# Two matmul stages of a convolution layer: groups of outputs in another turn, operands prepared tile by tile, block sums on VectorE

## The chip, the cores and the metric

One core of a Trainium2 chip. The metric is the device time of one launch in microseconds (us). TensorE is PE, VectorE DVE, ScalarE ACT, GpSimd POOL; SyncE (SP) only issues DMAs, and so does ACT's queue for some stores.

## What is computed

One layer over 2048 tokens of width 1024, float32, DEPTH = 1, so the mixer is the short convolution:

```python
h = modulate(rms_norm(x, norm_gains[i, 0]), sh_m, sc_m)   # shift, scale, gate from c @ ada_w
bcv = h @ w_in; gate_b, gate_c, v = jnp.split(bcv, 3, axis=-1)
h = (gate_b * conv3(gate_c * v)) @ w_out                  # three taps, causal, per channel
x = x + g_m * rms_norm(h, norm_gains[i, 1])
h = swiglu(modulate(rms_norm(x, norm_gains[i, 2]), sh_f, sc_f))   # w_gate_up, silu(g)*u, w_down
x = x + g_f * rms_norm(h, norm_gains[i, 3])
```

## The kernel before

**Stages.** The tokens are two halves u = 0, 1 of 1024. Each half goes through four matmul stages: `in` (w_in), `out` (w_out), `gu` (w_gate_up), `down` (w_down). The order in the program is in0, out0, in1, out1, gu0, down0, gu1, down1. `in1` does not read what `out0` makes: it is the other half of the tokens.

**Seven products.** A stage works in groups of outputs. A group is a 2 by 2 block product (two quarters of 512 tokens by two blocks of output columns, each over two halves of the inner dimension) done with seven products P1 to P7 in place of eight. The left operands are sums of quarters: A11, A12, A22, S1, S2, S3, S4 (`FEATURES`, line 40). The right ones are sums of weight blocks 11, 12, 21, 22. Each operand is split in two parts: a rounded one ("high", on ACT, type fp32r) and the rest ("low", on VectorE), and a product of 128 inner rows is three matmuls of 128x512. A group's product is a slot: 12 matmuls, in `out` 9 + 3 for P1 and P2. `slots` is the order of all of them, and everything else is hung on slot numbers: a list of events (`schedule`), chores that come back (`later`, `run`), and the supply of weights (`supply`, lines 830 to 844), which runs ahead of the products by so many places: 9 for the loads of blocks, 7 for their sums, 5 for the high part, 4 for the low part, 5 for weights kept whole (line 31). All engines run in the order in which the program was written.

**Weights.** In `in0`, the groups of feature blocks j = 1 and 2 also store their seven split operands in DRAM; `in1` reads them back whole ("kept") for these j and makes those of j = 0 and 3 again from blocks ("unkept"). In `gu0` and `gu1` the first three of 22 groups are kept, the other 19 unkept. `Blocks.sum` (lines 319 to 328) makes the four block sums of an unkept group; they run on POOL (`G`), those of the first three groups of `in0` on VectorE (`V`). While `in` runs, the weights of three groups of `gu` are prepared too (`Between`).

**Order of groups.** A group of `in` is one of c, C, b (the two input halves of the gated product, and the output gate) for a j. `in1` takes j in the order 1, 2, 0, 3, three groups each; the first three groups go in lockstep, the rest one after another. When group b of a j is done, `sums` (lines 650 to 667) forms S1 to S4 of the convolution's result on VectorE and POOL and stores all seven operands of that j in DRAM (`y_d`), tile k = j of four.

**Operands.** `loaded` (lines 747 to 778) brings the operands of `out` and `down` back: a DMA 6 slots before the first use, the high part 4, the low part 3 before. `normalized` (lines 730 to 745) makes those of `in1`, `gu0` and `gu1` from x: load, scale by the norm's factor (VectorE), shift (ACT), sums and splits, each as one instruction over four tiles (128x2048) where it can.

**Chores near the change.** `norm_of_rows` loads x again by rows (tiles `xr`, 16 loads of 256 KB for `in1`), squares on ACT; it starts 66 and 40 slots before `in1`. `mods_later((2, 3), ...)` loads `ada` tiles (32 of 256 KB) and reduces each against silu(c) on VectorE; it starts 8 slots into `out0`, one step every 1.25 slots. `after_out` computes x + gate * norm during the next stage (tiles `zz`, `xx`, and `nq` on POOL). SBUF is held in pools by tile size: 16 tiles of 8 KB per partition, 13 of 2 KB for raw blocks, 9 temporaries (line 32); a DMA or an instruction that fills a tile waits for the last user of that buffer.

Of the kernel before, what the change touches and what calls it, by code (L numbers as in the profile page):

```python
# [13 lines left out]
ALU = mybir.AluOpType  # L14
# [17 lines left out]
NBIG, NWP, NRAW, NTMP, NRB = 16, 7, 13, 9, 2  # L32
# [14 lines left out]
def hybrid_conv_layer(  # L47
# [255 lines left out]
    class Blocks:  # L303
# [193 lines left out]
    class Group:  # L497
# [85 lines left out]
        def ready_b(self, c):  # L583
# [12 lines left out]
            if {"12", "21"} <= self.done:  # L596
                run(sums(t, y_d[ph.u], self.i, f"{self.name}s"))
# [52 lines left out]
    def sums(t, d, k, name):  # L650
# [12 lines left out]
        store(("S2", s2))  # L663
# [23 lines left out]
    class Features:  # L687
# [59 lines left out]
    def loaded(ph, slots, first):  # L747
# [61 lines left out]
    for s in slots:  # L809
# [5 lines left out]
        else:  # L815
            b = of.setdefault((ph.name, s.n), Blocks(ph.kind, s.grp, ph.name == "in0" and s.n < LEAD))
# [404 lines left out]
    for ph in phases[1:]:  # L1221
# [28 lines left out]
    schedule(first["out0"] + 8, lambda: run(mods_later((2, 3), 1.25)))  # L1250
# [88 lines left out]
```

## Time and profile before

| | |
|---|---|
| Three runs | 2028.06, 2029.80, 2031.02 us, median 2029.8 us |
| The profiled execution | 2027.7 us, of which the span from the first to the last instruction is 2025.9 us |
| PE busy | 1949.8 us (96%), 8460 matmuls |
| VectorE, ScalarE, POOL busy | 71%, 43%, 33% |
| Granted TensorE clock, mean | 0.988 of full |
| DMA | 463.19 MB, mean 229 GB/s |

PE counts as busy also while its clock is low, so what a stretch loses is seen from its number of matmuls rather than from its busy time. In names, `in0P` is a PSUM bank of stage in0, `in7P` a pair of split weights of group 7's weights, `in7b` raw blocks of it, `out0S` an operand S of out0; numbers at the end of names are left out, and so S1 to S4 read alike. Almost every instruction goes through one helper, so its line is L75.

### The profile page before, as it was taken

How to read it: one execution, taken by the hardware profiler on the slowest of the kernel's cores; microseconds unless marked ns; L12 is line 12 of the kernel's file. 1: busy time of each engine (PE TensorE's matmuls, PEld its weight loads, DVE VectorE, ACT ScalarE, POOL GpSimd, SP SyncE). 2: the span in 40 equal slices, each digit the busy share in tenths (PEclk: the TensorE clock that was granted, in tenths of full speed). 3: DMA queues.
4: the chain of work that ended last, by engine and by line, in shares of the span. 5: the costliest groups of instructions: out<-in, count | busy, mean ns of one | idle time of the engine just before them, and what ended most of it. 6: DMA issues, size and time to landing. Idle time of an engine off the chain costs nothing.

```text
span 2025.9 us, 25058 instructions
## 1 busy us (share of the span) xinstructions
PE 1949.8 (96%) x8460; PEld 1583.4 (78%) x8460; DVE 1436.3 (71%) x1894; ACT 862.8 (43%) x1394; POOL 668.6 (33%) x436
## 2 busy tenths in 40 slices
PE   5899998999889999999999999999999999999998
PEld 2578786778777778887888888887888888888886
DVE  5887887887989685698757656667767555565456
ACT  5533446633333653343333435544333333344452
POOL 0134531302542233357856421111444343311010
PEclk9999998999999999999999999999999999999999
DMA  9269959879766775477656788567746234185644
GB/s 392 73 262 343 353 189 352 318 258 344 240 221 213 277 270 187 140 232 252 227 184 219 258 278 308 197 247 258 224 158 222 94 122 138 68 310 214 208 148 148
DMA packets 206193, 463.19 MB, mean 229 GB/s; under 512 B 23024, under 2 KB 38512, under 8 KB 199152
## 3 DMA queue, kind: packets, MB, share of 16 engines
q1 hardware_dynamic: 178416, 396.18, 56.5%
q10 hardware_dynamic: 27648, 65.41, 8.5%
q8 instruction: 66, 1.08, 0.2%
q14 instruction: 63, 0.52, 0.1%
HBM read 328.33 MB, written 133.17 MB: 228 GB/s over the span
## 4 chain that ended last, share of the span: by engine, by line
PE 72%; DVE 13%; DMA 7%; issue 4%; ACT 3%; SPq 0%; POOL 0%; ACTq 0%; POOLq 0%; DVEq 0%
PE gu1P L75 20%; PE gu0P L75 16%; PE down0P L75 10%; PE down1P L75 9%; PE in0P L75 7%; PE in1P L75 6%; PE out0P L75 2%; PE out1P L75 2%; DVE zz L75 1%; DMA xr<-x_d 1%; DMA xx<-xt_d 1%; DVE xx L75 1%; DVE ada L75 1%; DVE gu0a L75 1%; DVE in1y L75 0%
## 5 line engine op out<-in xcount | busy, mean ns | idle before, releaser
L75 DVE TENSOR_TENSOR gu1a<-gu1P,gu1a 128x512 f32<-128x512 f32 x63 | 43.4, 690 | 93.6 <-PE gu1P L75 86.8
L75 DVE TENSOR_TENSOR gu0a<-gu0P,gu0a 128x512 f32<-128x512 f32 x63 | 43.2, 688 | 60.4 <-PE gu0P L75 55.4
L75 POOL TENSOR_TENSOR down0q<-down0q,down0q 128x512 f32<-128x512 f32 x14 | 26.0, 1855 | 154.4 <-ACT down0q L75 154.3
L75 POOL TENSOR_TENSOR down1q<-down1q,down1q 128x512 f32<-128x512 f32 x10 | 16.1, 1613 | 148.6 <-ACT down1q L75 148.5
L75 ACT COPY gu1a<-gu1P 128x512 f32<-128x512 f32 x42 | 24.5, 586 | 89.8 <-PE gu1P L75 78.3
L75 DVE CUSTOM_DVE_ANT_0 ada<-ada,c 128x512 f32<-128x512 f32 x80 | 62.5, 791 | 0.2 <-ACT c L75 0.2
L75 ACT COPY gu0a<-gu0P 128x512 f32<-128x512 f32 x42 | 24.5, 584 | 72.4 <-PE gu0P L75 64.6
L75 ACT COPY gu1g<-gu1P 128x512 f32<-128x512 f32 x24 | 14.1, 587 | 90.9 <-PE gu1P L75 90.9
L75 POOL TENSOR_TENSOR gu1a<-gu1a 128x512 f32<-128x512 f32 x11 | 19.5, 1774 | 89.6 <-DVE gu1g21s L75 24.7
L75 DVE TENSOR_TENSOR gu1g<-gu1P,gu1g 128x512 f32<-128x512 f32 x24 | 16.6, 690 | 45.1 <-ACT gu1g L75 43.8
L75 POOL TENSOR_TENSOR nq<-nq,nq 128x512 f32<-128x512 f32 x28 | 46.5, 1660 | 2.6 <-ACT nq L75 2.4
L75 ACT COPY gu0g<-gu0P 128x512 f32<-128x512 f32 x24 | 14.1, 586 | 73.3 <-PE gu0P L75 73.3
L75 POOL TENSOR_TENSOR out1q<-out1q,out1q 128x512 f32<-128x512 f32 x14 | 24.1, 1724 | 59.1 <-ACT out1q L75 59.0
L75 DVE TENSOR_TENSOR gu0g<-gu0P,gu0g 128x512 f32<-128x512 f32 x24 | 16.6, 690 | 32.2 <-ACT gu0g L75 31.6
L75 POOL TENSOR_TENSOR out0q<-out0q,out0q 128x512 f32<-128x512 f32 x14 | 24.8, 1768 | 42.6 <-ACT out0q L75 42.5
L75 DVE TENSOR_TENSOR xx<-xx,zz 128x512 f32<-128x512 f32 x32 | 35.8, 1120 | 3.5 <-DMA xx<-xt_d 2.6
L75 POOL TENSOR_TENSOR gu0a<-gu0a 128x512 f32<-128x512 f32 x11 | 19.5, 1774 | 48.7 <-DVE gu0g11s L75 8.0
L75 POOL TENSOR_TENSOR in3b<-in3b,in3b 128x512 f32<-128x512 f32 x4 | 9.6, 2389 | 77.9 <-DMA in3b<-w_in_d 63.9
L75 ACT ACTIVATE gu0a<-gu0a 128x512 f32<-128x512 f32 x42 | 26.6, 633 | 15.5 <-DVE gu0a L75 14.2
L75 ACT ACTIVATE gu1a<-gu1a 128x512 f32<-128x512 f32 x42 | 26.6, 633 | 14.7 <-DVE xo L75 7.7
L75 DVE TENSOR_TENSOR down2P<-down2P,down2P 128x512 fp32r<-128x512 f32 x14 | 11.1, 796 | 28.6 <-ACT down2P L75 28.6
L75 ACT ACTIVATE nq<-xx 128x512 f32<-128x512 f32 x32 | 20.2, 631 | 25.0 <-DVE xx L75 21.4
(3215 smaller groups left out, 7007.4 us busy)
## 6 DMA issues: line engine op xcount, KB each, us to landing
ada<-ada_d SPq DMA_DIRECT2D x64, 256.0 KB, 5.1
act0A<-gu0a SPq DMA_DIRECT2D x33, 256.0 KB, 4.2
act1A<-gu1a SPq DMA_DIRECT2D x33, 256.0 KB, 3.2
ada<-ada_d SPq DMA_DIRECT2D x16, 512.0 KB, 8.2
zz<-z SPq DMA_DIRECT2D x32, 256.0 KB, 4.1
xx<-xt_d SPq DMA_DIRECT2D x32, 256.0 KB, 4.4
x<-xx ACTq DMA_DIRECT2D x32, 256.0 KB, 4.0
down0S<-act0S SPq DMA_DIRECT2D x8, 1024.0 KB, 7.1
```

The lines of the kernel that those rows point to most:

```text
L75: return tc.keep_in_program_order(f(*args, **kwargs))
```

## The change

- `Blocks.sum` runs on VectorE for all groups: 212 sums of 128x512 leave POOL (POOL has 212 instructions fewer, VectorE 212 more of this kind).
- `in1` takes its groups in another turn: j = 1; then c of 0 and 2, C of 0 and 2, b of 0 and 2; then j = 3. So kept and unkept groups alternate in groups 3 to 8.
- The last tile of S2 for `out0` and `out1` is not stored and read back: its high and low parts are written right from where `sums` makes it (`own`, `stay`). The other three tiles are loaded 8 slots before the first use instead of 6, split 5 and 4 before.
- In `normalized`, A11, A12, S3 and S2 are made tile by tile (`upper`), with the low part in two instructions (`lower`), A11 and A12 one to three slots earlier, d's scaling two slots later.
- The row norms for `in1` start 84 and 58 slots before it (before 66 and 40), the `ada` chore for m = 2, 3 starts 2 slots before `out0` (before 8 after) with a step per slot.
- Pools: 17, 15 and 10 tiles in place of 16, 13 and 9, with a smaller scratch area for dynamic DMA.

```diff
-NBIG, NWP, NRAW, NTMP, NRB = 16, 7, 13, 9, 2
+NBIG, NWP, NRAW, NTMP, NRB = 17, 7, 15, 10, 2
...
         def sum(self, op):
-            b, E = self.b, V if self.opening else G
+            b = self.b
             if op in ("P7", "P6") and "T3" not in self.summed:
                 self.summed.add("T3")
-                E.tensor_tensor(b["12"], b["22"], b["12"], ALU.subtract)
+                V.tensor_tensor(b["12"], b["22"], b["12"], ALU.subtract)
...
-                self.groups = [(f, j) for j in ((0, 1, 2, 3), (1, 2, 0, 3))[u] for f in ("c", "C", "b")]
+                turn = ((0,), (1,), (2,), (3,)) if u == 0 else ((1,), (0, 2), (3,))
+                self.groups = [(f, j) for js in turn for f in "cCb" for j in js]
...
-                run(sums(t, y_d[ph.u], self.i, f"{self.name}s"))
+                run(sums(t, y_d[ph.u], self.i, f"{self.name}s", self.n == len(ph.groups) - 1 and stay[ph.u]))
...
-        store(("S2", s2))
+        if own:
+            own["upper"](s2)
+            later(1, partial(own["lower"], s2))
+        else:
+            store(("S2", s2))
...
+        def upper(self, op, shift=False, less=None):
+            t, name = self.t[self.SOURCE[op]], self.ph.name + op
+            A_ = self.ph.A[op, 0] = big(name + "h", F32R), big(name + "l", F32R)
+            for k4 in range(4):
+                if shift:
+                    self.shift(self.SOURCE[op], (k4,))
+                if less:
+                    a, b = (self.t[x] for x in less)
+                    V.tensor_tensor(t[:, k4, :], a[:, k4, :], b[:, k4, :], ALU.subtract)
+                A.copy(A_[0][:, k4, :], t[:, k4, :])
...
-            ("P1", -12, partial(f.load, "a")), ("P1", -8, partial(f.scale, "a")), ("P1", -7, partial(f.shift, "a")),
-            ("P1", -6, partial(f.high, "A11")), ("P1", -5, partial(f.low, "A11")),
+            ("P1", -12, partial(f.load, "a")), ("P1", -9, partial(f.scale, "a")),
+            ("P1", -8, partial(f.upper, "A11", True)), ("P1", -7, partial(f.lower, "A11", (0, 1))),
+            ("P1", -6, partial(f.lower, "A11", (2, 3))),
...
+                if ph.kind == "out" and op == "S2":
...
+                    def upper_of(s2, tiles_of=tiles_of):
+                        A.copy(tiles_of()[0], s2)
...
+                    stay[ph.u].update(upper=upper_of, lower=lower_of)
+                    k = slice(0, KD // 2 - 1)
+                    schedule(first + n - 8, partial(load, k=k))
+                    schedule(first + n - 5, partial(upper, k))
+                    schedule(first + n - 4, partial(lower, k=k))
+                    continue
...
-                schedule(f - 66 + 26 * tok, lambda g=g, tok=tok: run(norm_of_rows(g, f"r{g}", partial(put, rb_in, tok))))
+                schedule(f - 84 + 26 * tok, lambda g=g, tok=tok: run(norm_of_rows(g, f"r{g}", partial(put, rb_in, tok))))
...
-    schedule(first["out0"] + 8, lambda: run(mods_later((2, 3), 1.25)))
+    schedule(first["out0"] - 2, lambda: run(mods_later((2, 3), 1)))
```

**How rows move.** SP's queue where `out0` begins, before (`y0S2` is the last S2 tile's store, `out0S20` the load of the whole of S2, `ada2` the loads of the chore, `kout` kept weights of `out`):

```order
L75 DMA y0S2_104<-in0b3s2_2485 128x512
L75 DMA out2P2_2547<-w_out_d 128x128
L75 DMA y0S3_105<-in0y3_2148 128x512
L75 DMA out3P2_2564<-w_out_d 128x128
L75 DMA out0A120_2359<-y0A12_101 128x512
L75 DMA c2_0_2574<-c_row_d 128x512
L75 DMA ada2_0_0_2576<-ada_d 128x512
L75 DMA xr321_2579<-x_d 128x512
L75 DMA y0S4_106<-in0b3s4_2486 128x512
L75 DMA out0P6_2592<-kout0P6_1174 128x512
L75 DMA ada2_0_1_2607<-ada_d 128x512
L75 DMA out1P6_2609<-kout1P6_1472 128x512
```

The next row there is `out0S20`, 128x2048. Now:

```order
L75 DMA y0S1_103<-in0b3s1_2537 128x512
L75 DMA out1P2_2586<-w_out_d 128x128
L75 DMA ada3_0_0_2592<-ada_d 128x512
L75 DMA out2P2_2609<-w_out_d 128x128
L75 DMA ada3_0_1_2615<-ada_d 128x512
L75 DMA y0S3_105<-in0y3_2183 128x512
L75 DMA out3P2_2630<-w_out_d 128x128
L75 DMA out0A120_2388<-y0A12_101 128x512
L75 DMA out0S20_2596<-y0S2_104 128x1536
L75 DMA y0S4_106<-in0b3s4_2539 128x512
L75 DMA ada3_0_2_2638<-ada_d 128x512
L75 DMA out0P6_2651<-kout0P6_1174 128x512
```

The store of the last S2 tile is gone, the load is of three tiles and stands 16 DMAs behind the first store of `in0`'s last result (22 before), and ten `ada` loads stand ahead of it (two before). Six of these ten stand ahead of that store.

VectorE in `in0` around group 7's weights (`in7P1` is the low part for P1), before:

```order
L75 TENSOR_TENSOR in7P1_1422<-in7b0_1315,in7P1_1422 128x512
L75 TENSOR_TENSOR in7P2_1443<-in7b3_1340,in7P2_1443 128x512
L75 TENSOR_TENSOR in6P3_1467<-in6b2_1218,in6P3_1467 128x512
L75 TENSOR_TENSOR in0b1_21_1289<-in0P7_5_1300,in0b1_21_1289 128x512
L75 TENSOR_TENSOR in0y1_1092<-in0b1_21_1289,in0y1_1092 128x512
```

Now:

```order
L75 TENSOR_TENSOR in7P1_1432<-in7b0_1319,in7P1_1432 128x512
L75 TENSOR_TENSOR in7b1_1401<-in7b2_1403,in7b1_1401 128x512
L75 TENSOR_TENSOR in7b0_1405<-in7b1_1401,in7b0_1405 128x512
L75 TENSOR_TENSOR in7P2_1456<-in7b3_1347,in7P2_1456 128x512
L75 TENSOR_TENSOR in6P3_1480<-in6b2_1218,in6P3_1480 128x512
L75 TENSOR_TENSOR in0b1_21_1293<-in0P7_5_1304,in0b1_21_1293 128x512
```

Two block sums stand between the two low parts, ahead of group 6's low part and of an eviction from PSUM (`in0b1_21<-in0P7`); both wait for blocks loaded two places earlier.

VectorE at the start of `in1`, before (`in1e` is S3, `in1a` becomes S2; an ISA row reduces an `ada` tile):

```order
L75 TENSOR_TENSOR in1S3l_3298<-in1e_3241,in1S3h_3272 128x2048
L75 TENSOR_TENSOR in1c_3105<-in1c_3105,in1d_3151 128x2048
L75 TENSOR_TENSOR in1a_2928<-in1c_3105,in1a_2928 128x2048
L75 ISA ada2_512_0_3207,ms2_1_2571<-ada2_512_0_3207,c2_1_3205 128x512
L75 ISA ms2_1_2571 128x1
L75 TENSOR_TENSOR in1c1_11_3268<-in1P2_0_3322,in1c1_11_3268 128x512
L75 TENSOR_TENSOR in1C1_11_3291<-in1P2_1_3340,in1C1_11_3291 128x512
L75 ISA ada2_512_1_3247,ms2_1_2571<-ada2_512_1_3247,c2_1_3205 128x512
```

Now:

```order
L75 TENSOR_TENSOR in1S3l_3310<-in1e_3308,in1S3h_3309 128x512 x4
L75 SCALAR_TENSOR_TENSOR in1d_3221<-in1d_3221,mA0_94,r3r_2548 128x512 x4
L75 TENSOR_TENSOR in1c_3166<-in1c_3166,in1d_3221 128x2048
L75 TENSOR_TENSOR in1c1_11_3338<-in1P2_0_3389,in1c1_11_3338 128x512
L75 TENSOR_TENSOR in1a_2971<-in1c_3166,in1a_2971 128x512 x4
L75 TENSOR_TENSOR in1C1_11_3357<-in1P2_1_3415,in1C1_11_3357 128x512
L75 TENSOR_TENSOR in1S2l_3406<-in1a_2971,in1S2h_3405 128x512 x2
```

The `ada` reductions of the second half have left this place (they now end ahead of `in1`'s S3), and the first eviction of `in1` stands ahead of S2's subtraction.

## Rows read from the trace of the kernel before

**Rows 1.** The page, part 1: busy time, share of the span and instructions of each engine.

```profile
PE 1949.8 (96%) x8460; PEld 1583.4 (78%) x8460; DVE 1436.3 (71%) x1894; ACT 862.8 (43%) x1394; POOL 668.6 (33%) x436
```

**Rows 2.** Stretches of the span, core 0: from and to, length, then busy us of PE, PEld, DVE, ACT and POOL, each with its number of instructions in brackets, then the granted clock, the DMA share and GB/s. From 150 to 200 TensorE never waits; the other stretches hold its waits.

```profile
100.00:150.00 50.00, 47.73 (x204) 39.00 (x203) 43.79 (x57) 18.91 (x33) 19.05 (x14) 0.97 0.66 250
150.00:200.00 50.00, 50.00 (x222) 41.38 (x222) 39.08 (x50) 17.29 (x31) 23.57 (x17) 1.00 0.93 344
310.00:332.00 22.00, 15.74 (x52) 11.34 (x52) 11.87 (x21) 13.78 (x25) 3.16 (x3) 0.77 0.98 362
388.00:416.00 28.00, 23.48 (x99) 18.61 (x98) 25.78 (x30) 15.87 (x19) 7.38 (x4) 0.94 0.78 290
524.00:556.00 32.00, 26.32 (x111) 20.78 (x110) 28.23 (x36) 13.34 (x24) 17.75 (x12) 0.95 0.72 243
570.00:590.00 20.00, 14.28 (x53) 10.98 (x53) 18.60 (x21) 6.22 (x12) 10.21 (x7) 0.83 0.46 145
660.00:678.00 18.00, 13.23 (x45) 10.13 (x44) 12.27 (x17) 11.33 (x18) 4.01 (x2) 0.81 0.89 331
930.00:945.00 15.00, 13.15 (x51) 10.42 (x50) 12.28 (x13) 3.40 (x6) 7.61 (x6) 0.89 0.77 264
```

**Rows 3.** TensorE's waits over the whole span: who waited for whom, us in total, times, the longest.

```profile
PE in1P L75 <- ACT in1c L75: 6.5, 2, 5.4
PE in1P L75 <- DVE in1c L75: 2.9, 1, 2.9
```

**Rows 4.** Timeline of `out0` around S2: start, duration, engine, operation, out<-in; in brackets the engine's idle time before and what ended it. SPq issues a DMA.

```profile
296.77 1.38 SPq L75 DMA_DIRECT2D y0A<-in0y  x2
311.31 0.60 SPq L75 DMA_DIRECT2D out0S<-y0S  x1
317.88 0.40 PE L75 MATMUL out0P<-out0A,out3P 128*128 128x512 f32 x1
320.32 1.90 ACT L75 CAST out0S20h<-out0S 128x2048 fp32r<-128x2048 f32 x1 [3.15 <-DMA out0S<-y0S]
322.25 2.29 DVE L75 TENSOR_TENSOR out0S<-out0S,out0S20h 128x2048 fp32r<-128x2048 f32 x1 [4.75 <-ACT out0S20h L75]
323.21 0.62 ACT L75 CAST out0P<-out0P 128x512 fp32r<-128x512 f32 x1
323.88 0.79 PE L75 MATMUL out0P<-out0S20h,out0P 128*128 128x512 f32 x1 [5.60 <-ACT out0P L75]
```

**Rows 5.** The same view of `out1` around S2.

```profile
645.93 0.93 SPq L75 DMA_DIRECT2D y1A<-in1y  x2
657.76 0.32 SPq L75 DMA_DIRECT2D out1S<-y1S  x1
664.22 0.39 PE L75 MATMUL out1P<-out1A,out3P 128*128 128x512 f32 x1
665.00 1.90 ACT L75 CAST out1S20h<-out1S 128x2048 fp32r<-128x2048 f32 x1 [3.13 <-DMA out1S<-y1S]
667.96 0.50 PE L75 MATMUL out1P<-out1S20h,out0P 128*128 128x512 f32 x1 [3.34 <-ACT out0P L75]
```

**Rows 6.** Timeline, VectorE and POOL from 302 us: three additions or subtractions of two tiles in SBUF, the last one while POOL's runs.

```profile
302.23 0.68 DVE L75 TENSOR_TENSOR in0b3s<-in0y 128x512 f32<-128x512 f32 x1
303.00 1.55 POOL L75 TENSOR_TENSOR in0y<-in0y 128x512 f32<-128x512 f32 x1 [28.64 <-DVE in0b3s L75]
303.30 1.79 DVE L75 TENSOR_TENSOR in0b3s<-in0b3s,in0y 128x512 f32<-128x512 f32 x1
```

**Rows 7.** Further stretches, columns as in Rows 2.

```profile
160.00:200.00 40.00, 40.00 (x178) 33.11 (x177) 29.74 (x38) 13.32 (x24) 17.66 (x13) 1.00 0.94 347
350.00:360.00 10.00, 10.00 (x45) 8.28 (x45) 7.86 (x10) 7.71 (x13) 2.60 (x2) 1.00 1.02 409
450.00:500.00 50.00, 50.00 (x220) 41.02 (x219) 35.42 (x62) 14.07 (x25) 7.95 (x6) 1.00 0.96 347
500.00:560.00 60.00, 54.32 (x233) 43.59 (x232) 55.99 (x72) 23.04 (x41) 33.72 (x22) 0.97 0.73 244
560.00:650.00 90.00, 82.55 (x356) 66.86 (x355) 83.43 (x131) 34.21 (x61) 30.18 (x20) 0.96 0.64 216
1000.00:1150.00 150.00, 150.00 (x663) 124.24 (x662) 97.52 (x103) 55.71 (x97) 91.59 (x63) 1.00 0.60 200
```

**Rows 8.** POOL's groups of instructions from 500 to 640 us, shapes and count, busy us, mean ns of one, idle time of POOL before them and what ended it: the first and the last of the six groups of block sums there, 22 sums in all.

```profile
L75 POOL TENSOR_TENSOR in1b<-in1b,in1b 128x512 f32<-128x512 f32 x4 | 6.8, 1695 | 11.0 <-DMA in1b<-w_in_d 8.4 <-DVE in1P L75 2.5
L75 POOL TENSOR_TENSOR in0b<-in0b,in0b 128x512 f32<-128x512 f32 x2 | 3.3, 1673 | 0.8 <-DVE in0P L75 0.8
```

**Rows 9.** Timeline, VectorE and POOL in `in0`: VectorE at the place of group `in7`'s first block sums, and POOL's first sum of that group.

```profile
182.41 1.28 DVE L75 TENSOR_TENSOR in7P<-in7b,in7P 128x512 fp32r<-128x512 f32 x2
187.24 1.29 POOL L75 TENSOR_TENSOR in7b<-in7b,in7b 128x512 f32<-128x512 f32 x1 [8.31 <-DMA in7b<-w_in_d]
```

**Rows 10.** POOL's groups in `gu0`, columns as in Rows 8: block sums of two neighbouring groups of outputs.

```profile
L75 POOL TENSOR_TENSOR gu11b<-gu11b,gu11b 128x512 f32<-128x512 f32 x4 | 5.9, 1481 | 7.4 <-DMA gu11b<-w_gu_d 7.2
L75 POOL TENSOR_TENSOR gu12b<-gu12b,gu12b 128x512 f32<-128x512 f32 x4 | 5.9, 1485 | 0.2
```

**Rows 11.** DMA issues: out<-in, issuing queue, count, KB each, median us to landing.

```profile
xr<-x_d SPq DMA_DIRECT2D x16, 256.0 KB, 4.7
```

**Rows 12.** VectorE's groups from 385 to 460 us, columns as in Rows 8.

```profile
L75 DVE CUSTOM_DVE_ANT_0 ada<-ada,c 128x512 f32<-128x512 f32 x15 | 11.1, 741 | 0.0
```

More of the change, by code (lines that the diff above doesn't have):

```diff
@@ L308, in hybrid_conv_layer, with __init__ @@
         FROM = {"11": 0, "12": 1, "22": 2, "21": 3, "11+": 0}
-        def __init__(self, kind, grp, opening=False):
+        def __init__(self, kind, grp):
             self.kind, self.grp, self.b, self.split, self.summed = kind, grp, {}, {}, set()
-            self.opening = opening
         def load(self, op):
@@ L468, in __init__ @@
             if ph.kind == "in":
-                self.grp = 3 * self.g.i + n % 3
+                self.grp = 3 * self.g.i + "cCb".index(self.g.what)
             else:
@@ L648, in store_operands, with sums @@
             SP.dma_start(d[o][:, k, :], src)
-    def sums(t, d, k, name):
+    stay = [{} for _ in range(NU)]
+    def sums(t, d, k, name, own=None):
         s1, s2, s4 = (tmp(f"{name}{i}")[:, :CH] for i in (1, 2, 4))
@@ L730, in normalized, with s3, lower @@
+        def s3(self):
+            self.t["e"] = big(f"{self.ph.name}e")
+            self.upper("S3", less=("a", "c"))
+        def lower(self, op, k4s):
+            t, (hi, lo) = self.t[self.SOURCE[op]], self.ph.A[op, 0]
+            for k4 in k4s:
+                V.tensor_tensor(lo[:, k4, :], t[:, k4, :], hi[:, k4, :].bitcast(F32), ALU.subtract)
     def normalized(f, at, early):
         for op, off, step in (
-            ("P1", -12, partial(f.load, "a")), ("P1", -8, partial(f.scale, "a")), ("P1", -7, partial(f.shift, "a")),
@@ L737, in normalized @@
+            ("P2", -10, partial(f.load, "b")), ("P2", -8, partial(f.scale, "b")),
+            ("P2", -7, partial(f.upper, "A12", True)), ("P2", -6, partial(f.lower, "A12", (0, 1))),
+            ("P2", -5, partial(f.lower, "A12", (2, 3))),
             ("P7", -11, partial(f.load, "c")), ("P7", -8, partial(f.scale, "c")), ("P7", -7, partial(f.shift, "c")),
-            ("P7", -6, f.s3), ("P7", -5, partial(f.high, "S3")), ("P7", -4, partial(f.low, "S3")),
-            ("P6", -12, partial(f.load, "d")), ("P6", -9, partial(f.scale, "d")), ("P6", -8, partial(f.shift, "d")),
@@ L740, in normalized @@
-            ("P6", -7, f.s1), ("P6", -6, f.s2), ("P6", -5, partial(f.high, "S2")), ("P6", -4, partial(f.low, "S2")),
+            ("P7", -6, f.s3), ("P7", -5, partial(f.lower, "S3", (0, 1))), ("P7", -4, partial(f.lower, "S3", (2, 3))),
+            ("P6", -12, partial(f.load, "d")), ("P6", -7, partial(f.scale, "d")), ("P6", -6, partial(f.shift, "d")),
+            ("P6", -6, f.s1), ("P6", -5, partial(f.upper, "S2", less=("c", "a"))),
+            ("P6", -4, partial(f.lower, "S2", (0, 1))), ("P6", -3, partial(f.lower, "S2", (2, 3))),
@@ L815, in hybrid_conv_layer @@
         else:
-            b = of.setdefault((ph.name, s.n), Blocks(ph.kind, s.grp, ph.name == "in0" and s.n < LEAD))
+            b = of.setdefault((ph.name, s.n), Blocks(ph.kind, s.grp))
             w = Weight(ph.kind, s.grp, s.op, b, ph.name == "in0" and s.g.i in (1, 2))
```

23 lines of the change are left out of this document (11 added, 12 removed).

## The prediction

> **What bounds the kernel now.** I read the page first: TensorE is busy 96% of the span, no other engine above 71% [rows 1]. So only time in which TensorE waits, or runs slowly after a wait, can be won. Busy time hides the second kind, so I counted matmuls by stretch: from 150 to 200 us there are 222 in 50 us, 0.2252 us each [rows 2]. By that measure a stretch loses its length less 0.2252 times its count: 10.3 us from 310 to 332 (52 matmuls), 5.7 from 388 to 416 (99), 7.0 from 524 to 556 (111), 8.1 from 570 to 590 (53), 7.9 from 660 to 678 (45), 3.5 from 930 to 945 (51), 4.1 from 100 to 150 (204) [rows 2]. Together 46.6 us. The granted clock there shows part of it: 0.77, 0.83 and 0.81 in the long stalls, so some matmuls ran at the lower level of 1.2 GHz after the idle time. Before 100 and after 2000 us there are losses too, which the change does not touch.
>
> Then the waits, and what ended last in each stretch. In `out0` TensorE finishes P2 at 318.3 and starts P6, the first user of S2, at 323.9, on a weight that ACT rounded at 323.2; ACT had stood behind the rounding of S2, which began at 320.3 when S2's load, issued at 311.3, had landed [rows 4]. `out1` repeats it: issue 657.8, rounding at 665.0, TensorE idle from 664.6 to 668.0 [rows 5]. In `in1` TensorE waits for ACT and VectorE to empty its PSUM banks, 6.5 us in two waits for c and 2.9 in one [rows 3], and VectorE is what is full: 56.0 of 60 us from 500 to 560 and 83.4 of 90 after it, against 35.4 of 50 just before [rows 7].
>
> **The change part by part.**
>
> *S2's last tile in `out0`.* The load goes from 22 to 16 DMAs behind the store at 296.8. Those 22 took 14.5 us [rows 4], 0.66 each, so it goes out at about 307.3. It moved 1 MB in 9.0 us (311.3 to 320.3); three quarters take 6.8, to 314.1; rounding three quarters of 1.90 us, to 315.5; the low part three quarters of 2.29, to 317.3. TensorE arrives at 318.3 [rows 4], so S2 no longer holds it. The last tile's rounding and subtraction come right behind its sum at 303.3 to 305.1 [rows 6], some 13 us early. Next late is S1: 14 DMAs behind S2's load (counted in SP's order), so issued at 316.5, landed at 325.5, ready at 329.7; TensorE wants it 48 matmuls after 318.3, at 329.1. I leave 1.8 us of the 10.3 for this and take **-8.5**; bounds -10.3, and 0 if the queue issues no sooner.
>
> *In `out1`* the load goes from 18 to 14 DMAs behind the store at 645.9; 18 took 11.8 us [rows 5], so it goes out at 655.1, lands after three quarters of 7.2 us at 660.5, is split at 663.6, before TensorE's 664.6. **-7.0** of 7.9, bounds 0 and -7.9.
>
> *Start of `in1`.* From 388 to 416 VectorE is busy 25.8 of 28 us [rows 2]. The `ada` chore puts 15 reductions, 11.1 us, between 385 and 460 [rows 12]; with its earlier start it ends before `in1`'s S3. A12 is ready two slots earlier, 5.4 us, and the waits here are shorter than that. Against it, more of the chore meets the scaling of A11 and A12 before 388. **-3.7** of 5.7; bounds -5.7, and +4 if VectorE falls behind before `in1`.
>
> *Turn of the groups in `in1`.* An unkept group costs VectorE seven low parts and now four sums, 11 of 0.68 us (the uncontended instruction of [rows 6]), 7.5 us. The three groups of j = 0 stood in slots 42 to 62 of `in1`; now they stand at 21, 35 and 49. So some 12.5 us leave the 60 us from 500 to 560 for the stretch before, which has 14.6 us free [rows 7]; 43.5 us of VectorE then stand in a stretch that would last 53. The loss of 7.0 there goes to about 1. From 560 on the three groups of j = 3 remain, but without the backlog; I take the 8.1 to 4. **-10** of 15.1; bounds -15.1 and +3 (two `b` groups now follow each other, and their sums want temporaries at once).
>
> *Block sums.* VectorE gets 212 of 0.68 us, and loses what POOL's took from it: an addition of two SBUF tiles takes 0.68 us alone and 1.79 while POOL's runs [rows 6], 1.1 us of hold-up. From 500 to 640 there are 22 such sums of about 1.7 us on POOL [rows 8]: 15.0 us added, at most 24.2 given back. Evictions from PSUM are not all held, so I take two thirds back, 16: neutral. Bounds for that stretch -9 and +15 us of VectorE. In `gu` VectorE is busy 97.5 of 150 us [rows 7], which hides 8 groups of 2.7 us there (22 us) even with nothing back: **0**, bounds -3.5 (the loss at 930) and +5.
>
> *What queues behind a sum.* POOL could wait for blocks alone; VectorE waits with evictions behind it. In `in0` VectorE reached that place of group 7 at 183.0 and POOL could begin at 187.2, when its blocks had landed [rows 9]. Two more raw tiles let SP load sooner, but the 16 `xr` loads [rows 11] start 49 us earlier, the first eight from 160 to 200, which already runs at 347 GB/s and 0.94 of the DMA engines [rows 7]. Eight of 256 KB are 2.1 MB; at 409 GB/s, the rate from 350 to 360 [rows 7], the 40 us have room for 62 GB/s, 2.5 MB, so they fit, barely. I charge `in0` **+3**; bounds -4.1 (its present loss) and +9 (two waits like group 7's reach TensorE).
> The Trainium skill ("SBUF — State Buffer", section "A bandwidth-pool intuition that's wrong") gives about 358 GB/s between HBM and a core. By it the stretch has room for 11 GB/s, 0.4 MB, and 1.7 MB would come late; the 409 GB/s of the row exceed it, so here the measurement decides.
>
> *Tile by tile.* S3 and S2 cost VectorE four times 0.68 in place of 2.29 [rows 4, 6], 0.4 us more each, in three stages; A11 is there sooner. The earlier start above covers it: 0; without that cover under 1 us a stage. The scratch area only makes room for tiles.
>
> Sum: -8.5 - 7.0 - 3.7 - 10 + 0 + 3 = -26.2 us. The profiled execution took 2027.7 us (span 2025.9 and 1.8 around it), which gives **2001.5 us**. It lies 2.1 us under the median of 2029.8, within the runs' own scatter of 3 us, so I leave it. About 0.2%, 4 us, is what a measurement of this kernel tells from no change.
>
> **The rivals.**
>
> *DMA takes half back.* Ten `ada` loads stand ahead of S2's load, and `out0` begins with 0.98 of the DMA engines taken [rows 2]. If S2, and then S1 behind six more, come late, `out0` wins 3.0 and not 8.5; if the `xr` loads delay blocks, `in0` costs 9 and not 3. 2001.5 + 5.5 + 6 = 2013.0. For it: the shares above. Against: the hole before 297, where SP waits for the store and six of the ten fit. Chance 0.20.
> By the Trainium skill's 358 GB/s (the same section) this would be the likelier case; the row of 409 speaks against it.
>
> *Everything goes.* All of 46.6 us would give 1981; with the late S1 and single waits left, 40 us, 1987.7. For it: each stall has its cause in the change. Against: VectorE stays near full from 560 to 650. 0.08.
>
> *Nothing.* What `in1` loses hangs on temporaries whose stores wait in SP's queue, and `out0` on S1; the stalls move and remain: 2026 to 2033. 0.06.
>
> *Slower: VectorE blocks on blocks.* 53 unkept groups now have VectorE wait for loads issued two places, 5.4 us, earlier. If each costs TensorE 0.7 us, that is 37.1 in place of the 3 charged: 2001.5 - 3 + 37.1 = 2035.6; from 0.55 us per group the gain is gone. For it: group 7 of `in0`, and `gu11`, where POOL waited 7.2 us for its blocks. Against: most groups of `gu` are like `gu12`, where POOL waited 0.2 us [rows 10], and VectorE has a third of its time free there. 0.10, and 0.01 for some other loss of this size.
>
> **How the numbers follow.** The forecast has 0.55: with its bounds 1992 to 2010. The range reaches to the better part of "everything goes" and to the far side of "DMA takes half back": **1985 to 2021**; left out are "nothing", "slower" and the ends, under 0.2. Faster by over 0.2%: 0.55 + 0.20 + 0.08 = 0.83; the same 0.06; slower 0.11.
>
> **What would show it.** Right: TensorE does not wait at P6 of `out0` and `out1`, with about 97 matmuls from 310 to 332 in place of 52; VectorE's share rises before 500 and falls after; POOL is busy some 310 us less (212 sums of about 1.48 us [rows 10]). Wrong: idle time on VectorE before block sums, ended by loads of `w_in_d` or `w_gu_d`, with TensorE waiting for evictions behind it; S1 late in `out0`; new waits in `in0` from 160 to 230; `in1` still losing over 10 us after 500.

## The result, and the profile after

The changed kernel takes **2000.2 us** (median of 4 runs, 1997.5 to 2003.2); the kernel before, run beside it, takes 2029.9 (2028.1 to 2031.0). The ratio is 0.9854, with an interval of 0.9838 to 0.9871: 29.7 us less, where 28.3 were forecast against the median. The profiled execution is the slowest of its four, 2003.2 us with a span of 2001.1; against the profiled one of before that is 24.5 us less, and the traces can explain only this much. By engines (answers to [rows 1]):

```profile
PE 1943.3 (97%) x8460; PEld 1581.3 (79%) x8460; DVE 1458.9 (73%) x2162; ACT 872.0 (44%) x1432; POOL 349.5 (17%) x224
```

POOL is busy 319 us less and VectorE 23 us more. The sums alone are told by the run sums_on_pool below, the same kernel with them on POOL: its VectorE is busy 1427.8 us, so 212 sums, 146 us at 0.69 each, cost 31 net. Most of their time came back, nearly as forecast, since POOL's additions run less beside VectorE's.

By stretch, columns as in [rows 2]. First six stretches of the kernel before, wide enough to take in whole stalls, since the change shifts these by some us:

```profile
0.00:100.00 100.00, 68.92 (x251) 42.15 (x252) 70.12 (x153) 55.13 (x90) 8.38 (x8) 0.95 0.61 235
196.00:222.00 26.00, 25.45 (x113) 20.75 (x112) 22.70 (x26) 9.08 (x16) 17.36 (x11) 1.00 1.02 385
310.00:346.00 36.00, 29.74 (x112) 22.57 (x112) 25.80 (x47) 22.97 (x41) 6.76 (x4) 0.86 0.95 352
376.00:424.00 48.00, 43.48 (x192) 35.31 (x191) 44.38 (x54) 24.28 (x29) 15.27 (x8) 0.96 0.84 316
560.00:640.00 80.00, 72.55 (x312) 58.57 (x311) 73.50 (x113) 31.32 (x55) 30.18 (x20) 0.96 0.68 230
640.00:678.00 38.00, 33.23 (x133) 26.70 (x132) 30.39 (x54) 15.96 (x30) 7.36 (x4) 0.91 0.73 256
```

The same of the changed kernel, with others that answer to [rows 2] and [rows 7]:

```profile
0.00:100.00 100.00, 68.49 (x241) 41.85 (x242) 68.40 (x151) 53.41 (x89) 2.60 (x6) 0.91 0.61 235
100.00:150.00 50.00, 48.75 (x215) 40.02 (x214) 46.14 (x68) 19.50 (x33) 9.29 (x6) 1.00 0.61 228
150.00:200.00 50.00, 50.00 (x222) 41.41 (x221) 37.53 (x62) 20.97 (x41) 8.14 (x6) 1.00 1.01 387
196.00:222.00 26.00, 21.95 (x87) 17.57 (x86) 17.17 (x29) 10.55 (x21) 7.77 (x6) 0.87 1.02 378
310.00:346.00 36.00, 31.38 (x126) 24.18 (x126) 27.63 (x53) 19.34 (x33) 8.10 (x5) 0.95 0.99 340
376.00:424.00 48.00, 41.91 (x178) 33.73 (x177) 44.26 (x66) 23.03 (x37) 16.67 (x9) 0.93 0.73 257
450.00:500.00 50.00, 50.00 (x220) 41.07 (x219) 41.09 (x69) 16.79 (x29) 4.71 (x3) 1.00 0.75 267
500.00:560.00 60.00, 60.00 (x269) 49.39 (x268) 55.55 (x89) 23.47 (x42) 14.73 (x10) 1.00 0.97 341
560.00:640.00 80.00, 80.00 (x358) 66.37 (x357) 75.23 (x128) 31.83 (x57) 15.09 (x11) 1.00 0.74 247
640.00:678.00 38.00, 38.00 (x168) 31.15 (x167) 29.63 (x46) 26.88 (x45) 8.17 (x5) 1.00 0.97 356
915.00:950.00 35.00, 32.40 (x140) 26.46 (x139) 30.08 (x39) 12.83 (x23) 18.26 (x12) 0.95 0.83 272
```

By the prediction's measure (length less 0.2252 us a matmul; narrow matmuls of the norms make it uncertain by about 1 us), the loss goes

| Stretch | before, us | after, us | change | forecast |
|---|---|---|---|---|
| ahead of 100 us (251 and 241 matmuls) | | | +2.3 | none |
| `in0`, 100 to 150 and 196 to 222 | 4.1 + 0.6 | 1.6 + 6.4 | +3.3 | +3 |
| `out0`, 310 to 346 | 10.8 | 7.6 | -3.2 | -8.5 |
| start of `in1`, 376 to 424 | 4.8 | 7.9 | +3.1 | -3.7 |
| `in1`, 500 to 640 | 17.3 | none left | -17.3 | -10 |
| `out1`, 640 to 678 | 8.1 | 0.2 | -7.9 | -7.0 |
| `gu0`, 915 to 950 (before: 930 to 945) | 3.5 | 3.5 | 0 | 0 |

The rows sum to -19.7 us of the 24.5. About 3 us more are won behind 678 us, outside the table, where nothing was forecast (norm_old below shows where), and the rest lies within the measure's uncertainty. That the total came out is in good part luck: `out0` and the start of `in1` gave 12 us less than forecast, `in1`'s middle 7 us more, and what lies outside the table made up some of the rest. The first two rows belong together, too: from 0 to 150 us the kernels have 455 and 456 matmuls, so what is won from 100 to 150 was lost ahead of it, and `in0` pays the whole stall of 5.8 us at 196 to 222.

VectorE's share rises before 500 (35.4 of 50 to 41.1), as said, but it does **not** fall behind it: 55.99 of 60 before, 55.55 after. It does that work beside 269 matmuls in place of 233.

Whom TensorE waits for now from 200 to 424 us, by the totals of its waits (us, times, longest; answers to [rows 3]). By the timeline, the first is the stall of `in0`, at 212.7; the second is for the first bank of `in1`, at 412.8; the third is for `out0`'s last evictions, at 385.5; the last is in `out0`, at 341.4, where ACT's copy comes behind the splitting of S1, for whose load ACT had stood 2.7 us:

```profile
PE in0P L75 <- ACT in0C L75: 4.0, 1, 4.0
PE in1P L75 <- DVE in1c L75: 3.4, 1, 3.4
PE out0P L75 <- DVE out0z L75: 2.1, 1, 2.1
PE out0P L75 <- ACT out0z L75: 1.4, 1, 1.4
```

The two long waits for ACT's copies of `in1` are gone, and so is the one at P6 of `out0` and `out1`. In `out0` (timeline; answers to [rows 4]) the first row is S2's last tile, split early; then S2's load and VectorE's queue at P2, with the waits of TensorE that follow:

```profile
314.85 0.68 DVE L75 TENSOR_TENSOR out0S<-in0b3s,out0S20h 128x512 fp32r<-128x512 f32 x1
313.48 0.41 SPq L75 DMA_DIRECT2D out0S<-y0S  x1
321.96 1.47 ACT L75 CAST out0S20h<-out0S 128x1536 fp32r<-128x1536 f32 x1 [0.57 <-DMA out0S<-y0S]
323.28 0.69 DVE L75 CUSTOM_DVE_ANT_0 ada<-ada,c 128x512 f32<-128x512 f32 x1 [1.85 <-DMA ada<-ada_d]
323.90 0.28 DVE L75 TENSOR_TENSOR out2P<-out2P,out2P 128x128 fp32r<-128x128 f32 x1
324.11 1.75 DVE L75 TENSOR_TENSOR out0S<-out0S,out0S20h 128x1536 fp32r<-128x1536 f32 x1
325.77 0.69 DVE L75 CUSTOM_DVE_ANT_0 ada<-ada,c 128x512 f32<-128x512 f32 x1
326.38 0.29 DVE L75 TENSOR_TENSOR out3P<-out3P,out3P 128x128 fp32r<-128x128 f32 x1
324.24 0.50 PE L75 MATMUL out0P<-out0A120h,out2P 128*128 128x512 f32 x1 [1.33 <-DVE out2P L75]
326.73 0.79 PE L75 MATMUL out0P<-out0A120h,out3P 128*128 128x512 f32 x1 [1.52 <-DVE out3P L75]
```

TensorE no longer waits for S2. It waits at P2 for the low parts of `out2P` and `out3P`: on VectorE an `ada` reduction, itself 1.85 us late for its load, stands ahead of the first, and another behind S2's low part ahead of the second.

### The profile page after: what moved, and what is told of

Same layout as the page of the kernel before. It is cut to its first block, busy times and chain, and to the rows that moved or that the text cites. A ratio compares the mean times of both kernels' runs of the same rounds, so it can differ in the third digit from the quotient of the medians.

```text
span 2001.1 us, 25050 instructions
## 1 busy us (share of the span) xinstructions
PE 1943.3 (97%) x8460; PEld 1581.3 (79%) x8460; DVE 1458.9 (73%) x2162; ACT 872.0 (44%) x1432; POOL 349.5 (17%) x224
## 4 chain that ended last, share of the span: by engine, by line
PE 79%; DVE 4%; DMA 4%; issue 3%; ACT 1%; SPq 0%; POOL 0%; POOLq 0%; ACTq 0%; DVEq 0%
PE gu1P L75 21%; PE gu0P L75 19%; PE in1P L75 11%; PE down0P L75 10%; PE down1P L75 9%; PE in0P L75 4%; PE out1P L75 4%; DMA ada<-ada_d 1%; PE out0P L75 1%; DVE in1c L75 0%; DMA x<-xx 0%; DVE down1z L75 0%; DMA out3P<-kout3P 0%; DMA in8b<-w_in_d 0%; DMA out2b<-w_out_d 0%
## 5 line engine op out<-in xcount | busy, mean ns | idle before, releaser
L75 DVE TENSOR_TENSOR gu1a<-gu1P,gu1a 128x512 f32<-128x512 f32 x63 | 43.5, 691 | 108.6 <-PE gu1P L75 108.6
L75 POOL TENSOR_TENSOR in0y<-in0y 128x512 f32<-128x512 f32 x4 | 5.7, 1435 | 139.5 <-issue 99.2
L75 DVE TENSOR_TENSOR xx<-xx,zz 128x512 f32<-128x512 f32 x32 | 28.0, 875 | 1.1
```

The lines of the kernel that those rows point to most:

```text
L75: return tc.keep_in_program_order(f(*args, **kwargs))
```

## Experiments

All are the changed kernel with the edit shown, save turn_raw, which is the kernel before with one part of the change. The kernel before gave 2030.0, 2030.3 and 2030.2 us beside the three groups of four. Medians of 4 or 5 runs; the intervals are about 3 us to either side, so differences under 3 us from the changed kernel's 2000.2 are not told from none. Where two intervals overlap, as with the changed kernel's and those of ada_late, rows_late, norm_old, ada_sums and turn_raw, the time alone decides nothing, and the traces must show the place.

| Run | us | ratio to before, interval | against 2000.2 |
|---|---|---|---|
| sums_on_pool | 1997.3 | 0.9834 (0.9820 to 0.9847) | -2.9 |
| old_turn | 2013.5 | 0.9919 (0.9905 to 0.9932) | +13.2 |
| s2_whole | 2011.1 | 0.9908 (0.9892 to 0.9925) | +10.9 |
| ada_late | 1995.3 | 0.9823 (0.9807 to 0.9839) | -4.9 |
| rows_late | 1995.4 | 0.9831 (0.9815 to 0.9847) | -4.8 |
| norm_old | 2004.8 | 0.9876 (0.9857 to 0.9895) | +4.6 |
| s1_after | 2000.6 | 0.9850 (0.9832 to 0.9869) | +0.4 |
| ada_sums | 1994.1 | 0.9832 (0.9814 to 0.9851) | -6.1 |
| ada_rows | 1991.7 | 0.9807 (0.9790 to 0.9823) | -8.5 |
| ada_rows_sums | 1994.3 | 0.9820 (0.9803 to 0.9837) | -5.9 |
| turn_raw | 2005.9 | 0.9879 (0.9859 to 0.9898) | +5.7 |
| pools_old | 2001.8 | 0.9856 (0.9838 to 0.9874) | +1.6 |

**old_turn.** The groups of `in1` in their old order.

```
-turn = ((0,), (1,), (2,), (3,)) if u == 0 else ((1,), (0, 2), (3,))
+turn = ((0,), (1,), (2,), (3,)) if u == 0 else ((1,), (2,), (0,), (3,))
```

> The changed kernel with in1's groups in the turn of before (j = 1, 2, 0, 3). Theory: the turn is the larger part of what in1 gained; VectorE's share from 450 to 500 falls and from 500 to 560 rises again, 8 to 13 of the 15 us from 500 to 650 come back, 2008 to 2013 us. Rival: the sums on VectorE and the larger pools did it; then in1 still waits for under 3 us and the time is 2000 to 2003.

13 us of the gain go with the turn. The two stretches of `in1` (columns as in [rows 2]) lose 6.2 and 5.8 us again:

```profile
500.00:560.00 60.00, 54.90 (x239) 43.61 (x238) 56.46 (x81) 25.21 (x45) 14.96 (x10) 1.00 0.86 283
560.00:650.00 90.00, 86.32 (x374) 70.13 (x373) 86.53 (x152) 36.18 (x64) 13.14 (x10) 0.98 0.68 221
```

**turn_raw.** The other way round: the kernel before, with the turn alone and the room that it needs.

```
-NBIG, NWP, NRAW, NTMP, NRB = 16, 7, 13, 9, 2
+NBIG, NWP, NRAW, NTMP, NRB = 16, 7, 15, 9, 2
...
-nc = bacc.Bacc("TRN2", target_bir_lowering=False, num_devices=1)
+nc = bacc.Bacc("TRN2", target_bir_lowering=False, num_devices=1, dynamic_dma_scratch_size=1024)
...
-self.groups = [(f, j) for j in ((0, 1, 2, 3), (1, 2, 0, 3))[u] for f in ("c", "C", "b")]
+turn = ((0,), (1,), (2,), (3,)) if u == 0 else ((1,), (0, 2), (3,))
+self.groups = [(f, j) for js in turn for f in "cCb" for j in js]
...
-self.grp = 3 * self.g.i + n % 3
+self.grp = 3 * self.g.i + "cCb".index(self.g.what)
```

> The kernel before with one part of the change alone: in1's groups in turn, j = 1, then 0 and 2, then 3. It needs two more raw tiles (15) and the small DMA scratch area that makes room for them; all else is as before, block sums on POOL, S2 whole. Theory A (the turn spreads VectorE's work and is worth 12 to 13 us by itself, as old_turn has it from the other side): 2017 to 2018, and in1 from 500 to 600 us loses 3 us or less in place of 15. Theory B (the turn needs the sums on VectorE or the operands tile by tile, since POOL's sums hold VectorE up): 2023 or more, with waits in in1 left.

It is worth more than either theory had: 24.3 us of the 29.7 come with the turn and two raw tiles, sums on POOL and S2 whole. By its trace some 17 of these lie in `in1` from 500 to 640 us, nearly 5 in `gu0` from 915 to 950 (160 matmuls for 139) and nearly 3 ahead of `in1`, which the turn does not touch, so a part may belong to the raw tiles. `in1` is full and `out0` much as it was before (60 matmuls from 310 to 332 us, [rows 2]: 52); what the second row loses is mostly `out1`'s wait for S2, which ends at 648.9:

```profile
500.00:560.00 60.00, 60.00 (x269) 49.45 (x268) 58.21 (x82) 24.09 (x43) 26.17 (x17) 1.00 0.99 340
560.00:650.00 90.00, 84.93 (x375) 69.21 (x373) 80.34 (x131) 35.42 (x64) 29.57 (x19) 1.00 0.75 254
```

VectorE is busier from 500 to 560 (58.2 of 60) than before, and TensorE waits nowhere. So a full VectorE was not by itself what cost `in1` time. Who waited there says more. Before, from 500 to 600 us, SP's queue (us in total, times, longest):

```profile
SPq L75 <- DVE xx L75: 33.8, 12, 6.7
```

Two of TensorE's waits before, each with the ACT row that it hangs on (timeline):

```profile
541.67 0.59 ACT L75 COPY in1C<-in1P 128x512 f32<-128x512 f32 x1 [5.16 <-DMA y1S<-in1b2s]
542.31 0.85 PE L75 MATMUL in1P<-in1S1h,in1P 128*128 128x512 f32 x2 [3.08 <-ACT in1C L75]
580.25 0.72 ACT L75 ACTIVATE in1y<-in1C,vt 128x512 f32<-128x512 f32 x1 [5.75 <-DVE in1C L75]
583.06 1.22 PE L75 MATMUL in1P<-in1S2h,in9P 128*128 128x512 f32 x2 [5.45 <-ACT in1c L75]
```

SP's queue in turn_raw:

```profile
SPq L75 <- PE in1P L75: 15.6, 7, 3.8
SPq L75 <- DVE xx L75: 11.8, 4, 4.9
```

So there are two routes. Before, SP stood 33.8 us for `xx`, a chore on VectorE, with stores and loads queued behind it; the stores of S2's parts (`y1S<-in1b2s`) went out late, the temporaries that they read came free late, and ACT's copy of the next product stood for them, TensorE behind it: the wait of 3.1 us at 542 and another of 1.6 at 555. The longest wait, 5.5 us at 583, went another way: ACT stood 5.8 us for VectorE's own work on a product (`in1C`), and the copy that TensorE needed came behind it on ACT. There VectorE itself was late, by its rows only 1.3 us of it for a load. With the turn SP's wait for `xx` falls to 11.8 us, SP waits mostly for TensorE to be done with a tile (it is ahead), and none of these three waits of TensorE is left. Which route the turn opened, or whether both, was not run apart, nor how much of the 24.3 is the two raw tiles. old_turn has them, no longer waits for those stores, and has its longest wait by the second route again (3.3 us, behind 5.9 of ACT for `in1C`); the tiles alone do not empty `in1`.

**pools_old.** `NBIG` 16 and `NTMP` 9 in place of 17 and 10; the 15 raw tiles stay.

> The changed kernel with 16 big tiles and 9 temporaries as before the change, in place of 17 and 10 (15 raw tiles stay). Theory A (the prediction's: more tiles only make room): 1999 to 2002. Theory B (the temporary is part of why in1's middle lost nothing at all, where the turn was given 10 of 15 us): in1 from 500 to 600 loses 2 us or more again, and the time is 2003 to 2005.

No difference that can be told, and 500 to 560 us hold 268 matmuls as before the edit. The larger pools of big tiles and temporaries are not why `in1` lost nothing.

**s2_whole.** S2 is stored and loaded whole again.

```
-..., f"{self.name}s", self.n == len(ph.groups) - 1 and stay[ph.u]))
+..., f"{self.name}s"))
...
-if ph.kind == "out" and op == "S2":
+if False:
```

> The changed kernel with the whole of S2 stored and loaded back, at the slots of before. Theory: out1 loses its 7 to 8 us again at P6; out0, which now waits at the second part of P2 already, loses 3 to 6 more; 2009 to 2014 us. Rival: the other edits (loads moved, pools) ended these waits; then 2000 to 2004.

The split is worth about 11 us. TensorE's wait for the weight behind S2's rounding is back in both stages (total, times, longest; `out0` from 310 to 345 us, `out1` from 645 to 670):

```profile
PE out0P L75 <- ACT out0P L75: 4.2, 1, 4.2
```

and in `out1`:

```profile
PE out1P L75 <- ACT out0P L75: 4.4, 1, 4.4
```

**ada_late.** The `ada` chore starts where it did before the change.

```
-schedule(first["out0"] - 2, lambda: run(mods_later((2, 3), 1)))
+schedule(first["out0"] + 8, lambda: run(mods_later((2, 3), 1.25)))
```

> The changed kernel with the ada chore where it was before (8 slots into out0, a step every 1.25 slots). Theory: the ten ada loads ahead of S2's load, and VectorE waiting for an ada tile ahead of low parts of weights, are what is left of out0's stall; out0 from 310 to 345 then loses 3 us in place of 7.6, the start of in1 1 to 4 more than its 6.5: 1996 to 2002 us. Rival: the early start is worth its while, the reductions meet in1's start; then over 2004.

The early chore cost some 5 us, and it bought nothing at the start of `in1`, where this kernel loses 5.2 us to the changed one's 7.9, although the reductions stand there again. `out0` loses 3.6, and its one long wait, 2.5 us, is for ACT's copy behind S1:

```profile
310.00:346.00 36.00, 32.93 (x144) 26.60 (x143) 27.65 (x45) 21.65 (x38) 7.27 (x4) 1.00 0.98 349
376.00:424.00 48.00, 43.96 (x190) 35.99 (x190) 44.54 (x68) 26.42 (x39) 11.36 (x7) 0.93 0.84 305
```

**rows_late.** The norms of rows, with their `xr` loads, 18 slots later, as before the change.

```
-schedule(f - 84 + 26 * tok, ...
+schedule(f - 66 + 26 * tok, ...
```

> The changed kernel with the row norms (the xr loads among them) back at their old place, 18 slots, some 49 us, later. Theory A (the stall of 6.5 us of in0 at 208 to 217 us is the xr loads' doing: they take DMA time from the blocks from 160 to 200): the stall falls to 3 us or less, 200 to 220 us hold 72 matmuls or more in place of 61, and the time is some 1996.5 us, if the later loads meet nothing in out0. Theory B (VectorE, which now stands and waits for blocks, is the cause, whoever delays them): the stall stays at 5 us or more and the time at 2000, or a little above, since out0 gets eight loads more. sums_on_pool brought it to 3.1, which fits both.

The stall of `in0` is gone without touching the sums, so theory A. `out0` pays part of it back: it loses 11.9 us in place of 7.6. From 150 to 200 us the DMA is as full as with the early loads, none of which stands there now:

```profile
150.00:200.00 50.00, 50.00 (x223) 41.40 (x222) 40.56 (x62) 19.27 (x34) 8.62 (x6) 1.00 1.00 376
196.00:222.00 26.00, 26.00 (x117) 21.53 (x116) 21.17 (x33) 11.03 (x20) 7.11 (x5) 1.00 1.03 396
310.00:346.00 36.00, 29.88 (x107) 21.67 (x106) 26.85 (x52) 22.71 (x40) 7.10 (x4) 0.86 1.00 362
```

**sums_on_pool.** The block sums on POOL, as before (`E` is VectorE only in the opening of `in0`).

```
-V.tensor_tensor(b["12"], b["22"], b["12"], ALU.subtract)
+E.tensor_tensor(b["12"], b["22"], b["12"], ALU.subtract)
...
```

> The changed kernel with the block sums back on POOL (those of in0's first three groups stay on VectorE). Theory: on VectorE the sums cost about what POOL's took from it, so the total stays at 1996 to 2004 us; the stall of 6.5 us in in0 from 208 to 217, where VectorE waits for the blocks of in8, goes to under 2, and in1 from 500 to 650 loses 2 to 8 us again, as POOL's sums hold VectorE up. Rival: the sums on VectorE are what emptied in1, then its 15 us come back and the time is over 2010. Second rival: they only cost, then 1994 or less with in1 still free of waits.

2.9 us faster, at the edge of what can be told. The stall of `in0` falls to 3.7 us, not under 2 as expected, and `in1` loses 1 us, not 2 to 8: moving the sums did not empty it. In `gu0` nothing is lost, where the changed kernel loses 3.5 us (140 matmuls):

```profile
915.00:950.00 35.00, 35.00 (x160) 28.93 (x159) 27.82 (x31) 14.66 (x27) 32.17 (x21) 1.00 0.79 273
```

That is no accident of one execution: in `gu0` TensorE waits 1.3 to 3.9 us for an ACT copy in every one of the nine kernels that have the sums on VectorE, and not at all in the four that have them on POOL with 15 raw tiles.

**ada_rows, ada_sums and ada_rows_sums.** The edits of ada_late, rows_late and sums_on_pool together.

> The changed kernel with both chores back at their old times: row norms 18 slots later, ada at out0 + 8. Alone they gave 1995.4 and 1995.3 against 2000.2. Theory A (each early chore costs where it stands: the xr loads in in0 at 208 to 217, ada's loads and reductions in out0): the two add up to 1990.5, with no stall at 208 to 217 and out0 losing 4 us or less. Theory B (what is taken out of one place comes down on the next: rows_late lost 12 us in out0 where the changed kernel lost 7.6): out0 loses 7 us or more again, and the time is 1994 to 1996.

> The changed kernel with two of its parts undone at once: the block sums on POOL and the ada chore at its old place. Alone they gave 1997.3 and 1995.3 against 2000.2, that is -2.9 and -4.9. Theory A (they cost in different stretches, in0 at 208 to 217 and out0): the two add up, 1992.4. Theory B (the sums on POOL slow VectorE down in out0, where ada's reductions now stand again in in1's opening): half of it, 1994 to 1996.

> As ada_rows, and the block sums on POOL as before the change; left of the change are the turn of the groups, S2's split, the operands tile by tile and the pools. By the theory that the sums on VectorE cost only where VectorE waits for late blocks (in0 at 208 to 217, which rows_late cured by itself), POOL's sums win nothing more: the same as ada_rows within 2 us. By the theory that they cost by their own time on VectorE: 2 to 3 us less than ada_rows, since sums_on_pool gave -2.9.

ada_rows is the fastest kernel of the case: 1991.7 us, faster than the changed one by 8.5, with an interval that does not meet the changed one's. In time the two add up nearly (9.7), in place they don't: `in0`'s stall is gone, `out0` still loses 6.7, more than ada_late's 3.6, so neither theory fits whole.

```profile
310.00:346.00 36.00, 33.36 (x130) 25.65 (x129) 28.53 (x50) 26.00 (x44) 6.79 (x4) 0.91 1.02 390
```

With `ada` or both chores back, POOL's sums win nothing that can be told (-1.2 and +2.6 us). So by time the sums cost nothing that can be told once the `ada` chore is back. In place they do: POOL's sums spare the wait in `gu0`, and `in1` from 560 to 640 us then loses 1.0 and 1.6 us, where ada_late loses nothing and ada_rows 0.3.

**norm_old.** The old table of `normalized`, with whole operands of 128x2048.

```
-("P1", -8, partial(f.upper, "A11", True)), ("P1", -7, partial(f.lower, "A11", (0, 1))),
+("P1", -7, partial(f.shift, "a")), ("P1", -6, partial(f.high, "A11")), ("P1", -5, partial(f.low, "A11")),
...
```

> The changed kernel with the old table of normalized's operands: whole operands of 128x2048 for A11, A12, S3 and S2, at the old slots. The prediction gave tile by tile 0 by itself, and put what in1's start was to win down to the earlier slots and the earlier ada chore; ada_late showed that the chore wins nothing there. Theory A (the table is worth something): the opening of in1, 388 to 420 us, loses 3 us or more beyond the 6.5 it has, gu0 1 to 2 more, and the time is 2003 to 2006. Theory B (the table is worth nothing, as the prediction's 0 has it): 1999 to 2001.

4.6 us slower by the median, but the two intervals overlap, and its profiled execution has a span of 2001.0, the changed kernel's 2001.1. At the start of `in1` it loses 7.7 us, the changed one 7.9. The place is the opening of `gu0` and `gu1`, where TensorE waits for VectorE to empty its first bank:

```profile
PE gu1P L75 <- DVE gu1a L75: 1.8, 1, 1.8
PE gu0P L75 <- DVE gu0a L75: 1.4, 1, 1.4
```

Of all the kernels run, the three with the old table (before, turn_raw, norm_old) have these two waits, of 1.4 to 1.8 us each, and the eleven with the new one have neither. So the table is worth a few us, in `gu`; by time alone that is not told.

**s1_after.** S1's sum one slot later, behind the eviction.

```
-("P6", -6, f.s1), ("P6", -5, partial(f.upper, "S2", less=("c", "a"))),
+("P6", -5, f.s1), ("P6", -5, partial(f.upper, "S2", less=("c", "a"))),
```

> The changed kernel with one entry of normalized's table moved by a slot: S1 (one VectorE instruction of 128x2048, 2.29 us) comes behind the eviction of the first product instead of ahead of it, in in0, in1 and gu0. Theory A (TensorE's wait of 3.4 us at 412.75 in in1's start is for the first product's bank, and the bank is held by the order on VectorE: shift on ACT, then S1, then the eviction): the eviction starts some 2.3 us or more earlier, in1's opening loses 4 us or less in place of 6.5, gu0 as much or 1 us less, and the time is some 1997. Theory B (what is late is S2's operand, made behind S1, and it would be TensorE's next wait): the wait changes its name and the time stays at 2000.

The time stays, as theory B has it, but what TensorE waits for next is not S2: its wait for the first bank falls from 3.4 to 0.6 us, and one for another bank takes its place (from 405 to 425 us):

```profile
PE in1P L75 <- DVE in1C L75: 2.6, 1, 2.6
PE in1P L75 <- DVE in1c L75: 0.6, 1, 0.6
```

## Why the prediction was right, and where its steps were not

- **The turn of `in1`** was taken at -10 and is -17 in the profile. The direction was right and the mechanism only half: the prediction took away from a full VectorE the work of three groups. The longest of TensorE's waits there did go over a late VectorE; the next two, 4.6 us, went from VectorE's chore over SP's queue and late stores to ACT's temporaries. The step that failed is that VectorE would have room: 43.5 us of work in a stretch of 53 were said, and VectorE stays full (55.55 of 60; for the 233 matmuls of before that is 48.1 us, an estimate from the two rows). TensorE was freed all the same, not because VectorE had time to spare; by which of the two routes above stays open. The prediction named the chain over the stores as its rival "nothing", as a reason that the stall would stay.
- **S2 in `out1`**: -7.0 forecast, -7.9 measured; its steps held.
- **S2 in `out0`**: -8.5 forecast, -3.2 measured. The queue did what was forecast: 9.9 us from the store at 303.57 to S2's load (10.5 said). The store itself came 6.8 us later than [rows 4], behind `in0`'s stall, and the load took 8.4 us, not 6.8, beside `ada`'s. What failed is that `ada` was counted on SP's queue alone, as loads, and not on VectorE, where its reductions stand ahead of weights' low parts: two waits, 2.8 us. S1's late load, for which 1.8 us were left, costs a wait of 1.4. The 3.0 us that the rival "DMA takes half back" gave `out0` are close to what was measured, and ada_late takes the loss from 7.6 to 3.6 us.
- **The start of `in1`**: -3.7 forecast, +3.1 measured. The step "the reductions leave this place, so it gets faster" fell with ada_late. A wait of 2.1 us at 385.5, for `out0`'s last evictions, stands behind the scaling of `in1b` and an `ada` reduction on VectorE, which the prediction had only as a bound ("+4 if VectorE falls behind before `in1`"). s1_after moved the next wait and another was there. VectorE is busy 44.3 of 48 us; what would shorten this start stays open.
- **`in0`**: +3 forecast, and the +3.3 of the table's `in0` row meets it by luck: against the 2.5 us won at 100 to 150 stand 2.3 lost ahead of 100. The stall alone is 5.8 us, within the bounds, and is the early `xr` loads' doing (rows_late). What was mis-sized is the room for them, taken from the 347 GB/s of before. The two more raw tiles, all of the change that turn_raw has in `in0` but for the scratch area, already fill the DMA: without any early `xr` load the DMA moves 376 GB/s from 150 to 200 us in rows_late and 375 in turn_raw, at a share of 1.00 and 0.99, against 344 at 0.93 before. With them it is 387 at 1.01, so there was next to no room, and VectorE stood 5.1 us for blocks of group 7 and up to 2.4 for those of group 8 (in rows_late under 1 us in all). The Trainium skill ("SBUF — State Buffer", section "A bandwidth-pool intuition that's wrong (but worth ruling out)") gives about 358 GB/s between HBM and a core. The 387 over 50 us exceed it, so its figure is not the limit here, though late blocks, which the prediction had worked out from it, did come.
- **Block sums**: 0 in `gu0` was forecast, and 3.5 and 3.5 us were measured, but these are two different waits. With the turn, the raw tiles and POOL's sums the one of before goes (turn_raw, sums_on_pool); with the sums on VectorE another comes. So a gain that nobody forecast hides a cost of the sums, 1.3 to 3.9 us of waiting, which the prediction put at nothing, within a bound of 5. It is far from the slower rival's 0.7 us a group.
- **Tile by tile**: 0 forecast; the two waits of `gu`'s openings are gone by it, 1.4 to 1.8 us each.
- **Its own signs of being wrong**: three came, VectorE idle before block sums of `in0`, S1 late in `out0`, a new wait in `in0`; and there were 72 matmuls from 310 to 332 us, not 97. The forecast held in its total, and in `out1`.

## What to carry to other kernels

Before pricing a stall by the engine that is full, follow each wait to what ended last: from 500 to 600 us turn_raw's VectorE is busier than before, and TensorE waits for nothing. A chore that is moved earlier is to be charged on every engine and queue at its new place (these two cost 8.5 us together), and room on the DMA is to be counted with all that the same change lets start sooner. A total that comes out says little of its terms: here a gain outside the forecast and three misses nearly made up for one another.

## What the runs showed of the hardware

VectorE's addition of two 128x512 tiles takes 0.69 us in the changed kernel, and 1.73 us where POOL works at the same time, as it does from 1045.6 to 1054.1 us (VectorE's groups from 1000 to 1050 us: shapes and count, busy us, mean ns; the first one begins at 1046.0):

```profile
L75 DVE TENSOR_TENSOR gu18b<-gu18b,gu18b 128x512 f32<-128x512 f32 x2 | 3.5, 1731 | 0.0
L75 DVE TENSOR_TENSOR gu17b<-gu17b,gu17b 128x512 f32<-128x512 f32 x4 | 2.8, 691 | 0.1
```

That was known from [rows 6]. What the DMA moves when it is full is not one number: 387 GB/s at a share of 1.01 from 150 to 200 us here, 376 at 1.00 in rows_late, and in the kernel before, from 20 to 50 us:

```profile
20.00:50.00 30.00, 23.34 (x87) 13.38 (x86) 21.35 (x52) 18.97 (x31) 1.38 (x1) 0.94 1.03 419
```

What sets the rate of such a stretch stays open.
